# Down projection of a decoder layer by seven half-size products, from forms of ff kept in DRAM

## The chip, the cores and the metric

The kernel runs on one core of one Trainium2 chip. The metric is the device time of one execution in microseconds (us): the median of three runs of the kernel before is 2154.42 us (2153.45 to 2158.33).

## The reference, cut to what matters

One layer (d_model 2048, 512 tokens, float32): a norm, three parallel mixers (attention, convolution, a gated recurrence), their common output projection and the residual; then the part that the change touches:

```python
h  = x + concat(mixers) @ w_out
n  = rms_norm(h, ffn_norm_w)
ff = silu(n @ w_gate) * (n @ w_up)          # 2048 -> 5632
y  = h + ff @ w_down                        # 5632 -> 2048
out = rms_norm(y, final_norm_w)
```

The output must agree in float32. One matmul in the fast format of TensorE keeps too few bits, so each operand is split into a high and a low part, and each product is three matmuls (high by high, high by low, low by high).

## The kernel before, in words

Everything after the mixers is held with channels as partitions and the 512 tokens as columns. The mixers end at about 600 us of the span. Four stages follow.

**Project** (`project`, L667). 16 tiles of `h` (128 channels x 512 tokens), each from 48 matmuls of 512 columns. Each tile is added to x on VectorE (DVE), stored to DRAM (`hd`) from ScalarE's queue, and split into `hh`, `hl` (scaled by ffn_w); GpSimd (POOL) adds up its squares in `acc`. `project_end` turns the sums into `rstd` and `rms`.

**Sums of n** (`token_sums`, L701). DVE builds four sums and differences of quarters of n, split as well; the seven half-size products of gate/up use them as the stationary operand.

**Gate/up.** ff has 44 tiles (128 channels x 512 tokens). The first two are computed plainly (`ff_plain`), the other 42 by Winograd's form of Strassen's scheme (`ff_fast`): seven products `11`, `12`, `S2`, `S1`, `S3`, `22`, `S4`, each 24 matmuls of 256 columns, in place of eight. A block of weights is a raw tile of 128 x 1024; ScalarE (ACT) casts it into `wh` (L136), DVE subtracts and gives `wl` (L137). The finished tile is stored to DRAM (`ffd`), 256 KB, on SyncE's queue (SP).

**Down** (`down_all`, L886). Five chunks of eight k-tiles and a last one of four. ACT's queue loads ff tiles from `ffd`, ACT and DVE split them (`fh`, `fl`), and each of 16 output tiles takes 24 matmuls of 512 columns per chunk, 1920 in all; DVE adds each to `h` (L813). The last chunk goes by halves of the tokens, 384 matmuls of 256 columns, with the final norm (`down_last`); POOL does a part of the last scaling (L860, L861).

The order on each engine is written down when the kernel is built, by a scheduler with priorities: what stands in `high_priority` is moved ahead as far as buffers allow. At run time each engine takes its list in order. A DMA is an entry of the list of the engine that issues it, and an entry that waits holds up all behind it.

Of the kernel before, what the change touches and what calls it, by code (L numbers as in the profile page):

```python
# [27 lines left out]
GF = 4  # L28
CF = 8
NCHUNK = NF // CF  # L30
PLAIN = 2
HALF = 256
NB = S // P
# [11 lines left out]
POOL_OUT = (0, 4)  # L45
# [8 lines left out]
def _layout_cols():  # L54
    at = 0
    for name, n in (
        ("attn_w", 16), ("q_w", 4), ("kv_w", 4), ("mla_w", 1), ("conv_w", 4 * CONV_W),
        ("conv_b", 4), ("ln_w", 4), ("ln_b", 4), ("lower", HG), ("hgrn_w", 1),
        ("ffn_w", 16), ("final_w", 16), ("inv_freq", 1), ("sign", 1), ("eps", 1),
        ("ln_eps", 1), ("half_pi", 1),  # L60
    ):
        _COLS[name] = (at, n)
        at += n
    return at
# [28 lines left out]
class Trunk:  # L93
# [573 lines left out]
    def project(self, w, r4):  # L667
# [3 lines left out]
        self.hd = self.dp.tile([KT, P, S], F32, name="hd")  # L671
        sq_sum = self.sq_sum = r4("acc")
        for m in range(KT):
            t = self.hf[:, m]
            nc.sync.dma_start(t, self.io["x"][m])
            bank = self.cols_tile(w, self.mix_y + self.mix)
            nc.vector.tensor_tensor(t, t, bank, op=ALU.add)
            nc.scalar.dma_start(self.hd[m], t)
            self.hw.append(self.split(t, self.hp("hh", F32R), self.hp("hl", F32R), self.col("ffn_w", m)))
            if m == 0:  # L680
                nc.scalar.activation(sq_sum, t, AF.Square)
            else:
                q = r4("sq")
                nc.scalar.activation(q, t, AF.Square)
                nc.gpsimd.tensor_tensor(sq_sum, sq_sum, q, op=ALU.add)
            nc.scalar.activation(t, t, AF.Copy, scale=self.col("ffn_w", m))

    def project_end(self, r4):
# [3 lines left out]
        y, q, v = r4("sq"), r4("sq"), r4("acc")  # L692
        nc.vector.tensor_scalar(self.rms, total, 1.0 / D, self.col("eps"), op0=ALU.mult, op1=ALU.add)
        r = self.rsqrt(total, D, "eps", v, y, q)
        nc.vector.tensor_scalar(self.epsv, self.rms, EPS, None, op0=ALU.mult)
        nc.vector.tensor_tensor(self.rms, self.rms, r, op=ALU.mult)
        nc.vector.tensor_copy(self.rstd, r)
# [28 lines left out]

    def put_ff(self, f, g, u):
# [4 lines left out]
        nc.sync.dma_start(self.ffd[f], u)  # L732

    def ff_plain(self, f, w, fp):
        nc = self.nc
        gbank = self.cols_tile(w, self.hw)
        ubank = self.cols_tile(w, self.hw)
        g, u = fp("g"), fp("u")
# [3 lines left out]
        nc.sync.dma_start(self.ffd[f], u)  # L742

    def ff_fast(self, f, w, rp, fp):
# [4 lines left out]
        with self.tc.high_priority(offset=6000):  # L749
            b11, b21, b12, b22 = raws = [rp("raw", F32, W) for _ in range(4)]  # L750
            for t in raws:
                nc.sync.dma_start(t, next(w))
# [19 lines left out]
        g, u = fp("g"), fp("u")  # L772
# [7 lines left out]
        def sums():  # L780
            tt(b11, b12, b11, op=ALU.subtract)
            t2 = rp("t2", F32, W)
# [16 lines left out]
        self.put_ff(f, g, u)  # L799


    def ff_load(self, k, fp):
        nc = self.nc
        with self.tc.high_priority(offset=3000):
            t = fp("fr")
            nc.scalar.dma_start(t, self.ffd[k])
            return self.split(t, fp("fh", F32R), fp("fl", F32R))

    def down(self, w, ff):
        nc = self.nc  # L810
        for m in range(KT):
            bank = self.cols_tile(w, ff)
            nc.vector.tensor_tensor(self.h[:, m], self.h[:, m], bank, op=ALU.add)  # L813

    def down_last(self, w, ff, r5, lp):

        nc = self.nc
        self.tables_after(self.last_silu)
        wt = []
        for m2 in range(KT // 2):  # L820
            if m2 < 3:
                h, l = self.weights(next(w))
                wt += [(h[:, :S], l[:, :S]), (h[:, S:], l[:, S:])]
            else:
                raw = self.wp.tile([P, 1024], F32, tag="raw", name="raw", bufs=2)
                nc.sync.dma_start(raw, next(w))
                for s in (slice(0, S), slice(S, 2 * S)):
                    wt.append(self.split(raw[:, s], lp("wlh", F32R), lp("wll", F32R)))
        n = S // 2
        acc = r5("acc")  # L830
        for th in range(2):
            ts = slice(th * n, (th + 1) * n)
            for m in range(KT):
                bank = self.ps("mm")[:, :n]
                for k in range(GF):
                    s = slice(k * P, (k + 1) * P)
                    self.mm3(bank, (wt[m][0][:, s], wt[m][1][:, s]), (ff[k][0][:, ts], ff[k][1][:, ts]),
                             k == 0, k == GF - 1)
                hm = self.h[:, m, ts]
                nc.vector.tensor_tensor(hm, hm, bank, op=ALU.add)  # L840
                if m == 0:
                    nc.scalar.activation(acc[:, ts], hm, AF.Square)
                else:
                    q = r5("sq", F32, (P, n))
                    nc.scalar.activation(q, hm, AF.Square)
                    nc.vector.tensor_tensor(acc[:, ts], acc[:, ts], q, op=ALU.add)
            scaled = {}
            for m in POOL_OUT:
                scaled[m] = o = lp("mx")
                for i in range(2):  # L850
                    nc.scalar.activation(o[:, i * n:(i + 1) * n], self.h[:, m + i, ts], AF.Copy,
                                         scale=self.col("final_w", m + i))
            bank = self.ps("ax")[:, :n]
            nc.tensor.matmul(bank, self.ones, acc[:, ts], start=True, stop=True)
# [255 lines left out]
```

## Time and profile before

| | |
|---|---|
| median of three runs | 2154.42 us |
| profiled execution, its own time | 2154.74 us |
| its span | 2153.0 us |
| PE busy | 2100.1 us (98%) |
| DVE busy | 1391.3 us (65%) |
| ACT busy | 891.2 us (41%) |
| POOL busy | 172.2 us (8%) |
| moved by DMA | 252.43 MB, 117 GB/s |

How to read it: busy time is summed over the instructions of an engine; PE is TensorE's matmuls. A busy share over the whole span mixes stages, so the table by stage below is the one to use. Instructions of one engine overlap a little at their ends, so a chain of n like ones takes less than n times the mean of one.

### The profile page before, as it was taken

The numbers are of one execution on the slowest core, as the hardware profiler recorded it, in microseconds if no ns is written. First come the engines' busy times: TensorE is split into PE (matmuls) and PEld (weight loads), VectorE is DVE, ScalarE is ACT, GpSimd is POOL, SyncE is SP. The second block draws the span as 40 slices with busy tenths as digits, with TensorE's granted clock in tenths as the row PEclk, the third lists the DMA queues.
The fourth block names the chain that finished last, engine by engine and source line by source line (L and its number), as shares of the span: only waits on it lengthen the run. The fifth ranks groups of instructions, "written<-read, shape, count | busy, mean of one in ns | idle before, by whom it ended". The sixth has DMA issues, their size and how long they took to land.

```text
span 2153.0 us, 31933 instructions
## 1 busy us (share of the span) xinstructions
PE 2100.1 (98%) x13060; PEld 1893.8 (88%) x13060; DVE 1391.3 (65%) x1787; ACT 891.2 (41%) x1353; POOL 172.2 (8%) x152
## 2 busy tenths in 40 slices
PE   8999999999999999999999999999997999999997
PEld 6888888878878789999999999999996788888887
DVE  7897785556543377777777778777776443443447
ACT  6324763457543344444444444444443222221223
POOL 4102474100011100000000000000000000000001
PEclk9999999999999999999999999999999999999998
DMA  5233422222153333433433433443335443342333
GB/s 186 96 118 98 143 80 87 90 83 79 63 187 122 123 122 114 133 111 111 133 116 106 133 122 104 128 129 106 120 123 181 137 137 103 132 135 94 100 107 98
DMA packets 89907, 252.43 MB, mean 117 GB/s; under 512 B 9424, under 2 KB 17872, under 8 KB 89760
## 3 DMA queue, kind: packets, MB, share of 16 engines
q1 hardware_dynamic: 76528, 228.00, 33.0%
q10 hardware_dynamic: 13120, 22.03, 2.9%
q8 instruction: 102, 1.67, 0.3%
q0 software_dynamic: 112, 0.36, 0.1%
q14 instruction: 45, 0.37, 0.1%
HBM read 226.24 MB, written 24.12 MB: 116 GB/s over the span
## 4 chain that ended last, share of the span: by engine, by line
PE 90%; ACT 3%; DVE 3%; DMA 2%; POOL 1%; issue 1%; SPq 0%; DVEq 0%; ACTq 0%; POOLq 0%
PE mm L145 28%; PE mm L146 28%; PE mm L147 28%; PE lv L374 1%; PE ob L615 1%; DMA xraw<-in_x 1%; PE lv L145 1%; PE lv L147 1%; PE lv L146 1%; DVE mx L866 1%; ACT wh L136 1%; DMA fr<-ffd 0%; PE tb L607 0%; POOL ps L364 0%; DMA raw<-in_w_down 0%
## 5 line engine op out<-in xcount | busy, mean ns | idle before, releaser
L136 ACT CAST wh<-raw 128x1024 fp32r<-128x1024 f32 (+1 forms) x463 | 478.2, 1034 | 834.7 <-PE mm L146 762.4
L137 DVE TENSOR_TENSOR wl<-raw,wh 128x1024 fp32r<-128x1024 f32 (+1 forms) x463 | 568.0, 1228 | 330.1 <-ACT wh L136 329.8
L146 PE MATMUL mm<-sl,wh 128*128 128x256 f32 x1344 | 378.3, 283 | 0.0
L145 PE MATMUL mm<-sh,wh 128*128 128x256 f32 x1344 | 378.1, 283 | 0.0
L147 PE MATMUL mm<-sh,wl 128*128 128x256 f32 x1344 | 373.5, 283 | 0.0
L145 PE MATMUL mm<-hh,wh 128*128 128x256 f32 (+1 forms) x1072 | 308.0, 287 | 0.0
L146 PE MATMUL mm<-hl,wh 128*128 128x256 f32 (+1 forms) x1072 | 307.5, 287 | 0.0
L147 PE MATMUL mm<-hh,wl 128*128 128x256 f32 (+1 forms) x1072 | 307.3, 287 | 0.0
L145 PE MATMUL mm<-fh,wh 128*128 128x512 f32 (+1 forms) x688 | 262.8, 386 | 12.8 <-ACT fh L136 9.7
L146 PE MATMUL mm<-fl,wh 128*128 128x512 f32 (+1 forms) x688 | 264.1, 384 | 0.2 <-DVE fl L137 0.2
L147 PE MATMUL mm<-fh,wl 128*128 128x512 f32 (+1 forms) x688 | 263.5, 383 | 0.0
L145 PEld LDWEIGHTS mm<-sh,wh 128*128 128x128 f32 x1344 | 257.3, 191 | 0.2 <-DVE u L794 0.2
L146 PEld LDWEIGHTS mm<-sl,wh 128*128 128x128 f32 x1344 | 257.5, 192 | 0.0
L147 PEld LDWEIGHTS mm<-sh,wl 128*128 128x128 f32 x1344 | 254.7, 192 | 0.0
L813 DVE TENSOR_TENSOR h<-h,mm 128x512 f32<-128x512 f32 x80 | 54.8, 687 | 236.2 <-PE mm L147 236.2
L146 PEld LDWEIGHTS mm<-hl,wh 128*128 128x128 f32 x1072 | 202.2, 189 | 3.0 <-issue 0.5
L145 PEld LDWEIGHTS mm<-hh,wh 128*128 128x128 f32 x1072 | 201.7, 188 | 3.4 <-issue 0.5
L147 PEld LDWEIGHTS mm<-hh,wl 128*128 128x128 f32 x1072 | 201.8, 188 | 2.9
L145 PE MATMUL mm<-xh,wh 128*128 128x512 f32 x400 | 160.1, 400 | 6.1 <-ACT wh L136 5.9
L145 PEld LDWEIGHTS mm<-fh,wh 128*128 128x128 f32 x688 | 130.4, 190 | 38.8 <-ACT fh L136 9.9
L146 PE MATMUL mm<-xl,wh 128*128 128x512 f32 x400 | 158.2, 396 | 0.5 <-DVE xl L140 0.5
L147 PE MATMUL mm<-xh,wl 128*128 128x512 f32 x400 | 157.0, 396 | 0.0
(330 smaller groups left out, 3236.6 us busy)
## 6 DMA issues: line engine op xcount, KB each, us to landing
raw<-in_w_gu SPq DMA_DIRECT2D x176, 512.0 KB, 4.2
raw<-in_w_down SPq DMA_DIRECT2D x88, 512.0 KB, 3.3
raw<-in_w_cols SPq DMA_DIRECT2D x42, 512.0 KB, 3.4
raw<-in_w_out SPq DMA_DIRECT2D x32, 512.0 KB, 3.3
ffd<-u SPq DMA_DIRECT2D x44, 256.0 KB, 3.8
fr<-ffd ACTq DMA_DIRECT2D x44, 256.0 KB, 3.7
raw<-in_w_rows SPq DMA_DIRECT2D x16, 512.0 KB, 3.3
raw<-in_w_attn SPq DMA_DIRECT2D x14, 512.0 KB, 3.4
```

The source lines that it names most:

```text
L136: nc.scalar.copy(h, src)
L137: nc.vector.tensor_tensor(l, src, h.bitcast(F32), op=ALU.subtract)
L145: mm(out, a[0], b[0], start=first, stop=False, **k)
L146: mm(out, a[0], b[1], start=False, stop=False, **k)
L147: mm(out, a[1], b[0], start=False, stop=last, **k)
L374: nc.tensor.matmul(bank[:, c * 64:(c + 1) * 64], e[:, c * P:(c + 1) * P], ap_of(e, c * P + h, [2 * h, 64 // h], [1, h]), start=True, stop= ...
L615: nc.tensor.matmul(obank[:, qs], pt[:, js], vt[h // 4, j][:, hs], start=j == 0, stop=j == i)
L813: nc.vector.tensor_tensor(self.h[:, m], self.h[:, m], bank, op=ALU.add)
L866: nc.vector.scalar_tensor_tensor(o[:, i * n:(i + 1) * n], self.h[:, m + i, ts], self.col("final_w", m + i), r, ALU.mult, ALU.mult)
```

## The change: what it does

`h` is now needed with tokens as partitions. In project, each `h` tile is transposed by four TensorE transposes (`turn`), copied by ACT and stored to `hd`; the gate tile of f = 0 stands ahead of `project_end`. In gate/up, two neighbouring ff tiles lie side by side in one tile `form`; `put_forms` makes of them the seven operands of down's products (four subtractions or additions of 128x256), casts them (`fh`, 128x1792) and takes the low part in place, and stores both, 0.92 MB each, where before two tiles of 256 KB were stored. The tiles `u`, `pb`, `g` and the raw tiles have other numbers of buffers.

Down is new (`down_all`, `down_block`). ff (tokens) is the stationary operand, w_down's sums move with 512 columns. Four chunks of 6, 6, 6 and 4 pairs of k-tiles, each done for two halves `mb` of the output: eight blocks of seven products. Per chunk the 14 tiles of forms are loaded by SP; per block 6 or 4 times n raw tiles of w_down (128x1024) come in, of which POOL and DVE make sums. The accumulators `acc` (four tiles of 128x2048) are loaded from `hd` by ACT's queue, and products are added into them by DVE. The final norm works on rows of tokens. In short:

```diff
     def project(self, w, r4):
         for m in range(KT):
-            t = self.hf[:, m]
+            t = r4("h")
             bank = self.cols_tile(w, self.mix_y + self.mix)
+            if m:
+                self.turn(m - 1, prev, r4)
             nc.vector.tensor_tensor(t, t, bank, op=ALU.add)
-            nc.scalar.dma_start(self.hd[m], t)
...
+    def turn(self, m, t, r4, tag="tb"):
+        bank = self.ps(tag)
+        for c in range(NB):
+            s = slice(c * P, (c + 1) * P)
+            nc.tensor.transpose(bank[:, s], t[:, s], self.ident)
+        o = r4("t")
+        nc.scalar.copy(o, bank)
+        nc.scalar.dma_start(self.hd[:, :, m * P:(m + 1) * P].rearrange("c p f -> p c f"),
+                            o.rearrange("p (c f) -> p c f", c=NB))
...
+    def put_forms(self, j, fp):
+        x = self.form
+        at = lambda i: x[:, i * HALF:(i + 1) * HALF]
+        tt = nc.vector.tensor_tensor
+        tt(at(4), at(1), at(3), op=ALU.add)
+        tt(at(1), at(0), at(1), op=ALU.subtract)
+        tt(at(5), at(4), at(0), op=ALU.subtract)
+        tt(at(6), at(2), at(5), op=ALU.subtract)
+        h = fp("fh", F32R, (P, 7 * HALF))
+        l = x[:].bitcast(F32R)
+        nc.scalar.copy(h, x)
+        tt(l, x, h.bitcast(F32), op=ALU.subtract)
+        for part, t in enumerate((h, l)):
+            nc.sync.dma_start(self.ffd[part, :, :, j * HALF:(j + 1) * HALF].rearrange("f p c -> p f c"),
+                              t.bitcast(F32).rearrange("p (f c) -> p f c", f=7))
...
+    def load_forms(self, at, n, tp):
+        with self.tc.high_priority(offset=3000):
+            for name in ("11", "12", "S2", "S1", "S3", "22", "S4"):
+                for part in range(2):
+                    t = tp(f"{name}{'hl'[part]}", F32R, (P, n * HALF))
+                    self.nc.sync.dma_start(t.bitcast(F32), self.ffd[part, FORMS[name], :, at * HALF:(at + n) * HALF])
...
+    def down_block(self, w, A, n, mb, rp, add, last=False):
+        product(one, b11, "11")
+        put((0, 0), one)
+        product(two, b21, "12")
+        put((0, 0), two)
+        def sums(i):
+            tg(b11[i], b12[i], b11[i], op=ALU.subtract)
+            t2 = self.wp.tile([P, 1024], F32, tag="raw", name="raw", bufs=2)
+            tv(t2, b22[i], b11[i], op=ALU.subtract)
+            tv(b21[i], t2, b21[i], op=ALU.subtract)
+            tg(b12[i], b22[i], b12[i], op=ALU.subtract)
+            return t2
+        product(one, Sums(), "S2", start=False)
...
     def run(self):
-        fp = area("gu", {"g": 2, "u": 2, "pa": 2, "pb": 2, "pc": 2}, "right")
+        fp = area("gu", {"g": 1, "form": 1, "fh": 1, "pa": 2, "pb": 1, "pc": 2}, "right")
-        rp = area("raw4", {"raw": 5, "t2": 1}, "right")
+        rp = area("raw4", {"raw": 4}, "right")
```

(`tg` is GpSimd, `tv` VectorE.) Three places where the lists of the engines change. The numbers behind names are buffer numbers; `L` is the line of the kernel that the row belongs to (in the new kernel the cast is L135 and its subtraction L136).

First, ACT's list at the start of down. Before, loads of `hd` and of ff and casts of ff alternate:

```order
L891 DMA h_16116<-hd_5009 128x512
L806 DMA fr_16150<-ffd_6188 128x512
L119 ACT_TABLE_LOAD
L806 DMA fr_16156<-ffd_6188 128x512
L136 CAST fh_16146<-fr_16144 128x512
```

Now the casts of the first nine raw tiles and the last pair's `fh` come, then the four loads of the accumulators, then the next casts:

```order
L770 CAST fh_16371<-form_15925 128x1792
L135 CAST wh_16515<-raw_16439 128x1024
L135 CAST wh_16531<-raw_16441 128x1024
L135 CAST wh_16547<-raw_16443 128x1024
L135 CAST wh_16570<-raw_16566 128x1024
L135 CAST wh_16591<-raw_16587 128x1024
L135 CAST wh_16612<-raw_16608 128x1024
L951 DMA acc_16392<-hd_5006 128x2048
L951 DMA acc_16393<-hd_5006 128x2048
L951 DMA acc_16394<-hd_5006 128x2048
L951 DMA acc_16395<-hd_5006 128x2048
L135 CAST wh_16630<-raw_16433 128x1024
```

The four accumulator loads now stand between the casts of product S2 and those of S1; `acc_16392` uses the memory of `form` and `fh`, so it comes after the two stores below.

Second, SP's list there. Before, the last ff tile is stored ahead of all but two of the weights of down:

```order
L732 DMA ffd_6188<-u_15660 128x512
L130 DMA raw_16319<-in_w_down 128x1024
L130 DMA raw_16351<-in_w_down 128x1024
L732 DMA ffd_6188<-u_15889 128x512
L130 DMA raw_16383<-in_w_down 128x1024
L130 DMA raw_16415<-in_w_down 128x1024
```

Now the stores of the last pair's two parts stand behind 12 raw tiles and the 14 loads of forms:

```order
L873 DMA raw_16455<-in_w_down 128x1024
L857 DMA 11h_16405<-ffd_6388 128x1536
L857 DMA 11l_16407<-ffd_6388 128x1536
L857 DMA 12h_16409<-ffd_6388 128x1536
L857 DMA 12l_16411<-ffd_6388 128x1536
L857 DMA S2h_16413<-ffd_6388 128x1536
```

```order
L857 DMA S4h_16429<-ffd_6388 128x1536
L857 DMA S4l_16431<-ffd_6388 128x1536
L773 DMA ffd_6388<-fh_16371 128x7x256
L773 DMA ffd_6388<-form_15925 128x7x256
L873 DMA raw_16832<-in_w_down 128x1024
```

Between these two pieces stand the other loads of forms; the two stores moved from the head of the queue to the end of these 26 loads.

Third, DVE's list in gate/up, where one ff tile ends and the next begins. Before (the first three rows are the subtractions of products 22 and S4, and of product 11 of the next tile):

```order
L137 TENSOR_TENSOR wl_11235<-raw_11068,wh_11234 128x1024
L137 TENSOR_TENSOR wl_11264<-raw_11070,wh_11263 128x1024
L137 TENSOR_TENSOR wl_11314<-raw_11296,wh_11313 128x1024
L794 TENSOR_TENSOR u_11080<-pc_11083,mm_11077 128x256
L781 TENSOR_TENSOR raw_11296<-raw_11298,raw_11296 128x1024
```

Now, at every second such place:

```order
L766 TENSOR_TENSOR form_9893<-form_9893 128x256
L136 TENSOR_TENSOR wl_10512<-raw_10345,wh_10511 128x1024
L767 TENSOR_TENSOR form_9893<-form_9893 128x256
L136 TENSOR_TENSOR wl_10541<-raw_10347,wh_10540 128x1024
L771 TENSOR_TENSOR form_9893<-form_9893,fh_10339 128x1792
L136 TENSOR_TENSOR wl_10589<-raw_10572,wh_10588 128x1024
L841 TENSOR_TENSOR g_10356<-pc_10360,mm_10355 128x256
L826 TENSOR_TENSOR raw_10572<-raw_10574,raw_10572 128x1024
```

The forms' work stands between the subtractions that the products wait for, and the wide one (L771) waits for ACT's cast `fh_10339`.

## Rows read from the trace of the kernel before

**Rows 1.** The page's chain that ended last, shares of the span

```profile
PE 90%; ACT 3%; DVE 3%; DMA 2%; POOL 1%; issue 1%; SPq 0%; DVEq 0%; ACTq 0%; POOLq 0%
```

**Rows 2.** By stretch: length, PE, PEld, DVE, ACT, POOL busy (count); clock, DMA, GB/s

```profile
570.00:746.00 176.00, 172.97 (x797) 143.45 (x795) 70.10 (x100) 74.68 (x128) 20.23 (x14) 0.99 0.40 136
800.00:1636.00 836.00, 835.98 (x7025) 835.78 (x7024) 635.32 (x707) 359.67 (x461) 0.00 (x0) 1.00 0.37 117
1637.00:1672.00 35.00, 22.01 (x81) 16.59 (x79) 23.12 (x35) 12.73 (x19) 0.00 (x0) 0.82 0.76 271
1672.00:2060.00 388.00, 388.00 (x1710) 321.10 (x1710) 157.40 (x177) 93.59 (x102) 0.00 (x0) 1.00 0.36 119
2137.00:2153.00 16.00, 0.70 (x2) 0.30 (x2) 9.02 (x18) 1.67 (x4) 3.56 (x4) 0.62 0.40 131
```

**Rows 3.** PE's waits, 1600 to 1700: released by; us, times, longest

```profile
PE mm L145 <- ACT fh L136: 9.7, 1, 9.7
PE mm L145 <- ACT wh L136: 3.0, 1, 3.0
```

**Rows 4.** Timeline of PE: start, us, what; project's mixers and stage ends

```profile
581.85 0.60 PE L639 MATMUL tb<-ident,og 128*128 128x128 f32 x4
582.29 0.27 PE L607 MATMUL tb<-ident,p 128*128 128x128 f32 x1
...
1314.31 0.28 PE L145 MATMUL mm<-hh,wh 128*128 128x256 f32 x1
...
1637.24 0.28 PE L147 MATMUL mm<-sh,wl 128*128 128x256 f32 x1
1647.26 1.65 PE L145 MATMUL mm<-fh,wh 128*128 128x512 f32 x3 [9.74 <-ACT fh L136]
...
2136.64 0.28 PE L147 MATMUL mm<-fh,wll 128*128 128x256 f32 x1
```

**Rows 5.** PE's waits, 740 to 800

```profile
PE mm L197 <- POOL acc L685: 4.0, 1, 4.0
```

**Rows 6.** DVE and ACT groups: shapes, count; busy us, mean ns; idle before

```profile
L137 DVE TENSOR_TENSOR wl<-raw,wh 128x1024 fp32r<-128x1024 f32 x447 | 552.8, 1237 | 329.3 <-ACT wh L136 329.1
L813 DVE TENSOR_TENSOR h<-h,mm 128x512 f32<-128x512 f32 x80 | 54.8, 687 | 236.2 <-PE mm L147 236.2
L794 DVE TENSOR_TENSOR u<-pc,mm 128x256 f32<-128x256 f32 x42 | 17.4, 414 | 0.0
L136 ACT CAST wh<-raw 128x1024 fp32r<-128x1024 f32 x447 | 469.0, 1050 | 833.9 <-PE mm L146 762.4 <-PE lv L147 26.1 <-PE mm L147 24.5
```

**Rows 7.** Timeline of DVE at an end of a gate/up tile

```profile
1309.76 1.23 DVE L137 TENSOR_TENSOR wl<-raw,wh 128x1024 fp32r<-128x1024 f32 x1 [1.42 <-ACT wh L136]
1312.87 1.23 DVE L137 TENSOR_TENSOR wl<-raw,wh 128x1024 fp32r<-128x1024 f32 x1 [1.89 <-ACT wh L136]
1314.02 0.41 DVE L794 TENSOR_TENSOR u<-pc,mm 128x256 f32<-128x256 f32 x1
```

**Rows 8.** The page's DMA issues: KB each, median us to landing

```profile
ffd<-u SPq DMA_DIRECT2D x44, 256.0 KB, 3.8
```

**Rows 9.** By stretch at down's start, columns as in rows 2

```profile
1644.00:1648.00 4.00, 0.74 (x2) 0.65 (x3) 1.08 (x2) 1.06 (x2) 0.00 (x0) 0.50 1.06 411
1652.00:1656.00 4.00, 4.00 (x17) 3.22 (x17) 4.00 (x8) 1.03 (x2) 0.00 (x0) 0.90 0.91 336
```

**Rows 10.** Timelines of DVE and POOL, early in the kernel and in project

```profile
24.86 2.43 DVE L140 SCALAR_TENSOR_TENSOR xl<-xraw,cols,xh 128x512 fp32r<-128x512 f32 x2
25.44 1.30 POOL L273 TENSOR_TENSOR acc<-acc,xsq 128x512 f32<-128x512 f32 x1 [2.26 <-ACT xsq L272]
27.82 0.74 DVE L140 SCALAR_TENSOR_TENSOR xl<-xraw,cols,xh 128x512 fp32r<-128x512 f32 x1
```

**Rows 11.** Timeline of the tail, after the last matmul

```profile
2142.17 6.71 DVE L866 SCALAR_TENSOR_TENSOR mx<-h,cols,v 128x256 f32<-128x256 f32 x12
2143.55 5.73 SPq L883 DMA_DIRECT2D out_y<-mx  x4
```

More of the change, by code (lines that the diff above doesn't have):

```diff
@@ L749, in ff_fast @@
         with self.tc.high_priority(offset=6000):
-            b11, b21, b12, b22 = raws = [rp("raw", F32, W) for _ in range(4)]
+            extra = lambda: self.wp.tile([P, 1024], F32, tag="raw", name="raw", bufs=2)
+            b11, b21, b12, b22 = raws = [extra()] + [rp("raw", F32, W) for _ in range(3)]
             for t in raws:
@@ new lines, in down_block, with load, early, parts @@
+    def down_block(self, w, A, n, mb, rp, add, last=False):
+        nc = self.nc
+        W = (P, 1024)
+        units = range(n // 2)
+        def load():
+            with self.tc.high_priority(offset=6000):
+                out = []
+                for _ in units:
+                    t = rp("raw", F32, W)
+                    nc.sync.dma_start(t, next(w))
+                    out.append(t)
+                return out
+        def early(f, *a):
+            with self.tc.high_priority(offset=6000):
+                return f(*a)
+        def parts(t):
+            h, l = (self.wp.tile([P, 1024], F32R, tag=x, name=x) for x in ("wh", "wl"))
+            return self.split(t, h, l)
+        def product(banks, ts, name, start=True, by_sub=False):
+            mine = A[name]
+            def step(b, hl, i, p):
+                s = slice(p * S, (p + 1) * S)
+                k = 2 * i + p
+                x = slice(k * HALF + b * P, k * HALF + (b + 1) * P)
+                self.mm3(banks[b], (mine[0][:, x], mine[1][:, x]), (hl[0][:, s], hl[1][:, s]),
+                         start and k == 0, k == n - 1, skip_group_check=not start)
+            if by_sub:
+                hls = [early(parts, ts[i]) for i in units]
+                for b in range(2):
+                    for i in units:
+                        for p in range(2):
+                            step(b, hls[i], i, p)
+                return
+            for i in units:
+                hl = early(lambda: parts(ts[i]))
+                for p in range(2):
+                    for b in range(2):
+                        step(b, hl, i, p)
+        b11, b21, b12, b22 = (load() for _ in range(4))
+        two_banks = lambda: [self.ps("mm") for _ in range(2)]
+        one, two, three, four = (two_banks() for _ in range(4))
+        def put(q, banks, op=ALU.add):
+            for b in range(2):
+                add(q, b, banks[b], op)
+        tv, tg = nc.vector.tensor_tensor, nc.gpsimd.tensor_tensor
+        product(one, b11, "11")
[9 more added lines that the diff above has]
+            return t2
+        class Sums:
+            def __getitem__(_, i):
+                return sums(i)
+        product(one, Sums(), "S2", start=False)
+        put((0, 1), one)
+        product(three, b11, "S1")
+        put((1, 1), three)
+        product(one, b12, "S3", start=False)
+        put((1, 0), one)
+        put((1, 1), one)
+        product(four, b21, "22")
+        put((1, 0), four, ALU.subtract)
+        product(three, b22, "S4", start=False, by_sub=last)
+        put((0, 1), three)
@@ L969, in run @@
         tp = area("sum", {"s": 1}, "right")
-        self.ffd = self.dp.tile([NF, P, S], F32, name="ffd")
-        wg = stream("w_gu")
+        self.ffd = self.dp.tile([2, 7, P, NP * HALF], F32, name="ffd")
         self.token_sums(sp, tp)
```

215 lines of the change are left out of this document (97 added, 118 removed).

## The prediction, made before the changed kernel ran

> **What bounds the kernel now.** I read the chain that ended last first: it is PE for 90% of the span [rows 1]. The table by stretch then says where PE still waits. In gate/up it never does, and its 7025 matmuls of 256 columns take 836 us, 0.119 us each; in the middle of down it doesn't either: 1710 matmuls of 512 columns in 388 us, 0.2269 us each; in project it works 173 of 176 us [rows 2]. It waits at the seams: 4.0 us for POOL's sum of squares ahead of the norm [rows 5], and at down's start 9.7 and 3.0 us [rows 3], with the clock granted at 0.50 (1.2 GHz) for a while after [rows 9]. So an edit counts here in two ways only: by how many matmuls PE is given, and by what it does to the seams. DVE is the second engine: 635 of 836 us in gate/up [rows 2].
>
> **The change part by part.** The sum is made against the profiled execution, 2154.74 us (0.3 above the median, 1.7 above its span).
>
> *Matmuls of down: -62.0.* Before, 1920 of 512 columns (435.6 us at 0.2269) and 384 of 256 (45.7 at 0.119): 481.3. After, 22 pairs x 7 products x 2 token tiles x 2 halves of the output x 3 = 1848 of 512 columns: 419.3. All on PE's path.
>
> *Transposes: +7.* 16 tiles by four. In the stream of matmuls before, four f32 transposes go by in 0.44 us (581.85 to 582.29 [rows 4]): 16 x 0.44 = 7.0. One by itself lasts 0.27 [rows 4], so unpipelined it would be 17.3; below 7 it can't go, since PE is full there. I take the pipelined end, because they stand between matmuls here too. ACT's copies and the stores lie beside PE's 11 us per tile.
>
> *The seam after project: +3 (-2 to +6).* The gate tile of f = 0 now stands ahead of the norm's sums and covers the 4.0 us. But `token_sums` also waits until the last transposed tile has been copied and stored (its memory is reused), some 9 us later by the new order, and the first fast product needs blocks that wait behind those sums. The two nearly cancel; I take +3.
>
> *Gate/up: +8 (0 to +40).* Per pair of tiles DVE gets four additions of 128x256 (0.41, [rows 6]) and one of 128x1792; by the shapes (1.237 at 1024, 0.414 at 256, so 0.0011 per element [rows 6]) the wide one takes about 2.05. That is 3.5 us more per 40, on 30: room in sum. The place matters. Before, the last subtraction of a tile (S4) starts 4.55 us ahead of the next tile's first matmul, and the next tile's first subtraction 1.44 us ahead [rows 4, 7]. Now two additions and the wide subtraction stand around S4's, and the wide one waits for ACT's cast of 1792 (1.05 x 1.75 = 1.8 us, [rows 6]), which starts only when the last addition is done, at about -4.5. So cast until -2.7, wide subtraction until -0.7, first subtraction of the next tile until +0.5, where the low part is wanted at about +0.2: PE waits some 0.4 us, in 20 pairs 8 us. If that cast is earlier it is nothing. The upper end: `form` has one buffer, and the next pair's first write to it (L839) waits for the landing of the low part's store, which is issued at the end of the wide subtraction, some 6.5 us earlier. A store of 256 KB lands after 3.8 us [rows 8]; 0.92 MB at 336 to 411 GB/s [rows 9] takes 2.2 to 2.7 us and lands after 5 to 6.6 by these rows. Just hidden; if not, some 2 us per pair.
>
> *Down's start: +24.9 (+18 to +32).* Before, from the last matmul of gate/up at 1637.24 to the last of down at 2136.64 are 499.4 us [rows 4], for 481.3 of work: 18.1 lost, nearly all at the start. Now count from gate/up's end, T = 0. SP's list there: 11 raw tiles that could not start earlier (5.77 MB, from about -4.8, when product 22 of the last tile lets go of memory), 14 forms (11.0 MB), the last pair's two stores (1.8 MB), all in one queue. At 375 GB/s, the middle of 336 and 411 [rows 9], the raws are through at 10.6, the first two forms at 14.8, with landing 17: PE stands still until T = 17 (before: 10.0). Then products 11 and 12, 16.3 us, a part of it at the lower clock. At that start before, the first three matmuls took 1.65 us [rows 4]; I take 2.5 us for it, so PE is done with both at 36. The third product, S2, adds onto the bank of the first, and that has to be put into the accumulator, which is loaded by ACT from `hd` only once both stores have landed: their memory is the accumulator's. 18.6 MB at 375 GB/s are through at 45, landed at 47; the first accumulator (1.05 MB) at 51.5, the second at 54.3; S2 starts at about 55. ACT, which issues those loads, stands still with them, so the casts for product S1 come late too, another 1.8. Lost: 55 less 16.3 of work, plus 2.5 for the lower clock once more after this second stand and the 1.8, is 43.0 against 18.1. At 336 GB/s S2 starts at 60, at 411 at 50.
>
> *The rest of down: +6 (0 to +25).* A block of n = 6 has PE for 252 x 0.2269 = 57.2 us. DVE has 21 subtractions and 6 sums of 128x1024 and 16 additions of 128x512: in a row, at 1.14 and 0.60 us (a tenth under the lone means of [rows 6]), 40.4 us. But POOL has six sums of 128x1024 there, and POOL gets in DVE's way: two operations that need 0.74 us each took 2.43 while POOL's 1.30 us addition ran [rows 10]. They take turns. POOL's for 1024 columns is about 2.6 (twice 1.30), so DVE and POOL in turn need 40.4 + 15.6 = 56.0 of 57.2; for n = 4 it is 30.1 + 10.4 = 40.5 of 38.1. The load is also uneven: until the last unit of S2 starts, 21.8 us into the block, 14 of DVE's (16.0), four additions (2.4) and four of POOL's (10.4) have to be done, 28.8. With three buffers for `wh` the work can start up to 5.4 us ahead, so 1.6 us too few per block at worst, and additions that read PSUM may not take turns. I take 0.8 for each of the seven blocks behind the first, whose long wait lets DVE run ahead.
>
> The Trainium skill says the same of that turn-taking ("SBUF — State Buffer", section "SBUF: two separate sides"): the ports which GpSimd shares with VectorE are held by one for a whole instruction, when VectorE has two inputs in SBUF. By that rule the trace agrees (2.43 for 1.48), and it speaks against giving POOL sums in down; it also leaves out the additions from PSUM, which would make the term the smaller one.
>
> *Tail: -1.7.* Before, 2153.0 - 2136.64 = 16.4 us. After: an addition (0.69), the small chain (2), eight scalings of 128x1024 at 1.14 (9.1) and a store of 512 KB (about 3): 14.7. The chain before was of the same kind: 12 scalings, and the stores among them [rows 11].
>
> Sum: 2154.7 - 62.0 + 7 + 3 + 8 + 24.9 + 6 - 1.7 = 2139.9, forecast 2140 us.
>
> **The rivals.**
>
> *A, the accumulators don't hold PE up.* If the stores or loads go sooner than their place in the queue says, S2 starts at 36, and 19 us of the loss are gone: 2121, and with the seams of gate/up hidden 2116. For it: transfers are spread over 16 engines, which before ran at a share of 1.06 at 411 GB/s [rows 9]. Against: the list of ACT has the loads ahead of the next casts, and the stores are last of 28 entries.
>
> *B, gate/up is held by its stores.* L839 comes just behind the landing. If the store, in pieces of 1 KB, takes 2 us longer than I reckon, every pair loses 2 us: 40 in place of 8, 2172. It decides from 1.1 us per pair (8 + 14.8 us in 20 pairs), slower than before beyond. For it: one buffer for `form` and `fh`, the margin is under 1.5 us. Against: traffic is low in gate/up, 117 GB/s [rows 2].
>
> *C, DVE and POOL in turn become the bound of down.* If also PSUM additions take turns, or the sums don't start ahead, a block loses up to 28.8 - 21.8 = 7 us; at 4 in seven blocks it is 28 in place of 6, 2162. It is slower than before from 2.9 us per block. For it: 56.0 of 57.2. Against: DVE in project is seen beside POOL only in small pieces, and PSUM reads may go free.
>
> **How the numbers follow.** What can be told from no change is 0.2%, 4.3 us: faster is under 2150.1, slower over 2158.7. Forecast 0.58 (own range 2126 to 2154), A 0.14, B 0.12, C 0.16. Faster: A and most of the forecast (0.50): 0.64. Same: 0.10, the forecast's upper edge and C's lower. Slower: B, C and the rest: 0.26. The range, 2117 to 2166, leaves out the far parts of B and C and half of A's lower end.
>
> **What would show it.** In project, four transposes per tile between matmuls, 0.44 us; if PE's gaps there grow, the first term is wrong. In gate/up, PE idle about 0.4 us per pair with the releaser `wl`; a wait of DVE for the landing of `ffd` at L839 would be B. At down's start, PE idle 17 us, working 19, then idle about 19 with the releaser an `acc` addition at L966, and ACT idle until the stores land; if the second gap is missing, A. In the blocks behind, PE idle for `wl` under 1 us per block; DVE subtractions stretched from 1.2 to over 3 us beside POOL, and PE waiting for them by several us in product S2, would be C. The forecast is wrong if PE's matmuls of down don't number 1848, or if the second gap is under 10 or over 30 us.

## The result, and the profile after

The changed kernel takes 2183.76 us (median of four runs, 2182.11 to 2185.25) against 2156.38 for the kernel before on the same chip: a ratio of 1.0125 (95% interval 1.0104 to 1.0146). The forecast was 2140, faster; it came out slower, above the range given. The profiled execution took 2185.25 us, its span is 2183.5. One execution of all the runs below was a slow one (2547.39 us, mean granted clock 0.748 where the others have 0.97 to 0.99), the profiled one of the first experiment, and no number below uses it.

The page of the changed kernel, first the busy times, then the chain that ended last, which answers to [rows 1]:

```profile
PE 2063.5 (95%) x12672; PEld 1842.1 (84%) x12672; DVE 1627.1 (75%) x1925; ACT 974.7 (45%) x1393; POOL 301.8 (14%) x188
PE 76%; DVE 10%; issue 5%; DMA 4%; ACT 3%; POOL 1%; SPq 0%; DVEq 0%; POOLq 0%; ACTq 0%
```

PE is busy 36.6 us less than before (2100.1), and yet the span is 30.5 longer. Its part of the chain fell from 90% to 76%, and DVE's rose from 3% to 10%: the end is now set by what PE waits for. The timeline of PE at the stage ends (start, duration, what) says where, set against [rows 4]:

```profile
803.40 0.28 PE L144 MATMUL mm<-hh,wh 128*128 128x256 f32 x1
1657.59 0.28 PE L146 MATMUL mm<-sh,wl 128*128 128x256 f32 x1
1672.75 0.77 PE L144 MATMUL mm<-wh,11h 128*128 128x512 f32 x1 [14.88 <-DMA 11h<-ffd]
1708.51 0.77 PE L144 MATMUL mm<-wh,S2h 128*128 128x512 f32 x1 [16.24 <-issue]
2167.68 0.39 PE L146 MATMUL mm<-wh,S4l 128*128 128x512 f32 x1
```

Between these starts and those of before:

| stretch | before | after | difference | predicted |
|---|---|---|---|---|
| start to the end of project | 745.7 | 755.1 | +9.4 | +7 |
| to the first matmul of 256 columns (the two plain tiles lie in it) | 51.6 | 48.3 | -3.3 | +3 |
| gate/up, the 42 fast tiles | 839.9 | 854.2 | +14.3 | +8 |
| down | 499.4 | 510.1 | +10.7 | -31.1 (-62.0 + 24.9 + 6) |
| tail | 16.4 | 15.8 | -0.5 | -1.7 |
| sum | 2153.0 | 2183.5 | +30.5 | -14.8 |

So 42 of the 45 us that the forecast was short lie in down. What PE waits for there, in the table of waits from 1640 to the end (us, times, longest), where before had the two waits of [rows 3]:

```profile
PE mm L145 <- DVE wl L136: 39.6, 16, 5.3
PE mm L144 <- issue: 16.2, 1, 16.2
PE mm L144 <- DMA 11h<-ffd: 14.9, 1, 14.9
```

The two long waits are those of down's start, and were predicted (17 and 19). The second of them is put down to "issue", where the profile shows nothing that PE waited for; DVE's timeline does, since the addition that frees the bank waited for the accumulators' loads:

```profile
1707.66 0.75 DVE L966 SCALAR_TENSOR_TENSOR acc<-acc,rms,mm 128x512 f32<-128x512 f32 x1 [13.01 <-DMA acc<-hd]
```

The first row of the waits is the new one: 39.6 us for DVE's subtractions. The stretches show it too (columns as in [rows 2]): the middle of gate/up, and the end of a block with the head of the next.

```profile
820.00:1620.00 800.00, 790.26 (x6638) 782.16 (x6637) 672.28 (x768) 374.18 (x452) 0.00 (x0) 1.00 0.46 151
1740.00:1800.00 60.00, 53.36 (x226) 43.34 (x224) 46.84 (x37) 19.84 (x19) 18.91 (x6) 0.94 0.51 181
```

In the second, PE stands for 6.6 of 60 us and its mean granted clock is 0.94, where [rows 2] had 1.00 and no idle time. DVE isn't full in it, 46.84 of 60. The timelines of DVE and of POOL in that stretch say why it is late all the same:

```profile
1752.05 0.67 DVE L968 TENSOR_TENSOR acc<-acc,mm 128x512 f32<-128x512 f32 x1
1752.65 2.82 DVE L925 TENSOR_TENSOR raw<-raw 128x1024 f32<-128x1024 f32 x1
...
1759.86 3.41 DVE L925 TENSOR_TENSOR raw<-raw 128x1024 f32<-128x1024 f32 x1
1763.20 3.40 DVE L926 TENSOR_TENSOR raw<-raw 128x1024 f32<-128x1024 f32 x1
1766.52 3.35 DVE L136 TENSOR_TENSOR wl<-raw,wh 128x1024 fp32r<-128x1024 f32 x1
...
1771.11 1.21 DVE L926 TENSOR_TENSOR raw<-raw 128x1024 f32<-128x1024 f32 x1
```

```profile
1748.64 2.40 POOL L923 TENSOR_TENSOR raw<-raw 128x1024 f32<-128x1024 f32 x1 [65.21 <-DVE wl L136]
1751.13 3.27 POOL L927 TENSOR_TENSOR raw<-raw 128x1024 f32<-128x1024 f32 x1
...
1762.16 6.64 POOL L927 TENSOR_TENSOR raw<-raw 128x1024 f32<-128x1024 f32 x2
```

POOL does its six sums in a row, in 20 us, once per block. In that time an operation of DVE with two inputs in SBUF takes up to 3.3 to 3.4 us in place of 1.2, just as long as one of POOL's: the two go in turn, one for one. The additions from PSUM (L968, 0.67) are not stretched, beside POOL or not. POOL's burst falls on the head of the block, where DVE has to give the sums and the low parts of two products. PE pays twice in each block of six pairs (the last row is the first place of the next block):

```profile
1758.86 0.50 PE L145 MATMUL mm<-wl,11h 128*128 128x512 f32 x1 [1.31 <-DVE wl L136]
1769.93 0.79 PE L145 MATMUL mm<-wl,12h 128*128 128x512 f32 x1 [5.33 <-DVE wl L136]
1825.28 0.50 PE L145 MATMUL mm<-wl,11h 128*128 128x512 f32 x1 [1.32 <-DVE wl L136]
```

A block lasts 66.4 us from one such place to the next (1758.86 to 1825.28; 65.7 to 66.9 in the others) for 57.2 of matmuls. 6.6 of the loss is waiting; most of the other 2.6 us is the lower clock behind the long wait, granted at 0.50 (1.2 GHz) for 3.4 us (columns as in [rows 2]):

```profile
1770.00:1773.40 3.40, 3.40 (x8) 2.72 (x9) 3.40 (x5) 0.00 (x0) 0.00 (x0) 0.50 0.00 0
```

### The profile page after: what moved, and what is told of

Read it like the earlier page. It is cut to its first block, busy times and chain, and to the rows that moved or that the text cites. A ratio compares the mean times of both kernels' runs of the same rounds, so it can differ in the third digit from the quotient of the medians.

```text
span 2183.5 us, 31515 instructions
## 1 busy us (share of the span) xinstructions
PE 2063.5 (95%) x12672; PEld 1842.1 (84%) x12672; DVE 1627.1 (75%) x1925; ACT 974.7 (45%) x1393; POOL 301.8 (14%) x188
## 4 chain that ended last, share of the span: by engine, by line
PE 76%; DVE 10%; issue 5%; DMA 4%; ACT 3%; POOL 1%; SPq 0%; DVEq 0%; POOLq 0%; ACTq 0%
PE mm L146 23%; PE mm L145 23%; PE mm L144 23%; DVE wl L136 4%; DMA ffd<-form 2%; DVE form L771 1%; ACT wh L135 1%; PE lv L373 1%; PE ob L614 1%; DVE raw L926 1%; DMA xraw<-in_x 1%; DVE raw L925 1%; PE lv L145 1%; PE lv L144 1%; PE lv L146 1%
## 5 line engine op out<-in xcount | busy, mean ns | idle before, releaser
L135 ACT CAST wh<-raw 128x1024 fp32r<-128x1024 f32 (+1 forms) x576 | 594.7, 1038 | 956.4 <-PE mm L145 425.3
L136 DVE TENSOR_TENSOR wl<-raw,wh 128x1024 fp32r<-128x1024 f32 (+1 forms) x576 | 731.2, 1278 | 351.4 <-ACT wh L135 347.5
L923 POOL TENSOR_TENSOR raw<-raw 128x1024 f32<-128x1024 f32 x22 | 66.8, 3040 | 1235.4 <-DMA raw<-in_w_down 903.4
L144 PE MATMUL mm<-mx,wh 128*128 128x512 f32 x256 | 101.0, 398 | 0.8 <-ACT mx L138 0.8
L146 PE MATMUL mm<-mx,wl 128*128 128x512 f32 x256 | 100.9, 395 | 0.0
L145 PE MATMUL mm<-mx,wh 128*128 128x512 f32 x256 | 100.8, 394 | 0.0
L144 PEld LDWEIGHTS mm<-xh,wh 128*128 128x128 f32 x400 | 76.5, 191 | 23.0 <-ACT wh L135 5.8
```

Of the source, the lines that this page charges most:

```text
L135: nc.scalar.copy(h, src)
L136: nc.vector.tensor_tensor(l, src, h.bitcast(F32), op=ALU.subtract)
L144: mm(out, a[0], b[0], start=first, stop=False, **k)
L145: mm(out, a[0], b[1], start=False, stop=False, **k)
L146: mm(out, a[1], b[0], start=False, stop=last, **k)
L923: tg(b11[i], b12[i], b11[i], op=ALU.subtract)
```

## The experiments

Theory 1: the loss per block comes from POOL and DVE taking turns at SBUF. Its rivals, as the expectations number them: theory 2, DVE has too much to do at the head of the block, whatever POOL does; theory 3, the raw tiles come late. A question apart from these is the second stand at down's start: does it come from the place of the last two stores in SP's queue, as predicted? T is the end of gate/up, as in the prediction. Runs given without an interval are single ones.

**All sums of w_down on DVE.**

```diff
-        tv, tg = nc.vector.tensor_tensor, nc.gpsimd.tensor_tensor
+        tv = tg = nc.vector.tensor_tensor
```

> Edit: all four sums of w_down's blocks on VectorE, none on GpSimd. Theory 1 (GpSimd and VectorE take turns at SBUF, so GpSimd's sums hold up the subtractions that PE waits for): the VectorE rows beside the sums fall from 3.3 to 1.2 us, the waits of PE for wl of 1.3 and 5.3 us per block go, the period of a block with n = 6 falls from 65.7-66.9 us to about 57.5, of n = 4 from 42.2 to about 38.5, the time to about 2184 - 5 x 8.7 - 2 x 4 = 2132. Theory 2 (VectorE has too much to do, unevenly, in the first three products, whatever GpSimd does): six more sums of 1.14 us at that place make the waits longer, period 70 us or more, time 2190 or more. Theory 3 (the raw tiles of w_down come late): nothing changes, 2184.

Measured: 2134.88 us (three executions), 0.9898 of before (0.9881 to 0.9915): 48.9 us less than the changed kernel, and faster than the kernel before by 1%. Theory 2 (2190 or more) and theory 3 (no change) are out by this. The trace is that of the same kernel, run once more:

> The kernel of e1 once more, for its profile. Theory 1 as there: period of a block with n = 6 about 57.5, VectorE's rows beside the sums 1.2 us, no wait of 1.3 and 5.3 us; time 2135.

2130.6 us (its part ahead of gate/up was some 7 us shorter than in the changed kernel, by chance: nothing differs there). Of PE's waits, one over 0.3 us is left in each block of six pairs, in product S2:

```profile
1759.04 0.50 PE L145 MATMUL mm<-wl,S2h 128*128 128x512 f32 x1 [0.85 <-DVE wl L136]
1817.81 0.50 PE L145 MATMUL mm<-wl,S2h 128*128 128x512 f32 x1 [0.84 <-DVE wl L136]
```

DVE by groups in this kernel, from 1710 to 2120 (count; busy us, mean ns; idle before):

```profile
L136 DVE TENSOR_TENSOR wl<-raw,wh 128x1024 fp32r<-128x1024 f32 x143 | 172.7, 1221 | 68.9 <-ACT wh L135 68.9
L925 DVE TENSOR_TENSOR raw<-raw 128x1024 f32<-128x1024 f32 x19 | 23.1, 1217 | 0.0
```

And the same groups in the changed kernel, from 1710 to 2167:

```profile
L136 DVE TENSOR_TENSOR wl<-raw,wh 128x1024 fp32r<-128x1024 f32 x145 | 203.9, 1412 | 92.4 <-ACT wh L135 90.6 <-DMA 22h<-ffd 1.5
...
L925 DVE TENSOR_TENSOR raw<-raw 128x1024 f32<-128x1024 f32 x19 | 45.4, 2389 | 0.5
```

With more work given to DVE the block is shorter, 58.8 in place of 66.4 us, and every operation is back at 1.22. From S2's start to the last matmul it is 414.4 us (1698.36 to 2112.75) in place of 459.2. The edit also changes the order of DVE's list and in which PE takes the products at the head of a block; the run with POOL's idle work, below, has the order of this one.

**Half of the sums back on POOL** (b11's on DVE, b12's on POOL).

```diff
-            tg(b11[i], b12[i], b11[i], op=ALU.subtract)
+            tv(b11[i], b12[i], b11[i], op=ALU.subtract)
```

> Edit: the first of the four sums (b11) on VectorE, the last one (b12, needed only for product S3) stays on GpSimd. Theory 1: half of GpSimd's time is gone, and the first product's chain no longer goes through GpSimd; the waits per n = 6 block fall to about 2 us, period about 60, time about 2145 to 2155. Theory 2: 2184 or more.

2164.87 us. In PE's waits in down the row of the subtractions is now this one:

```profile
PE mm L145 <- DVE wl L136: 23.7, 12, 2.4
```

It lies between the two, as the theory has it, but the time is 10 us over the upper end. A block takes 62.8 to 64.3 us. Three of POOL's operations in place of six take away a third of the loss per block, not half or more; why is not shown.

**POOL does work that nobody reads**: the sums on DVE as above, and two subtractions of 128x1024 per unit on POOL, into a tile of its own.

```diff
-        tv, tg = nc.vector.tensor_tensor, nc.gpsimd.tensor_tensor
+        tv = tg = nc.vector.tensor_tensor
...
+            for _ in range(2):
+                nc.gpsimd.tensor_tensor(self.junk, b22[i], b22[i], op=ALU.subtract)
```

> Edit: e1 (all sums on VectorE), and beside it two additions of 128x1024 per unit on GpSimd, as many as GpSimd had in the change, whose result nobody reads. Theory 1 (turns at SBUF): PE's waits for wl at the head of each block come back although nothing waits for GpSimd's results; time 2165 to 2195 (e1: 2135). Theory 1b (the chain through GpSimd's sums is what is late: 3.3 us each, handed on to t2 and the split of S2): the waits stay away, 2135 to 2140.

2180.75 us: 46 of the 49 us are back, though nothing waits for POOL's results and the lists at the head of the block are in the order of the kernel without POOL's work. PE, DVE and POOL of this kernel, each from its timeline:

```profile
1829.16 0.80 PE L145 MATMUL mm<-wl,11h 128*128 128x512 f32 x1 [7.61 <-DVE wl L136]
```

```profile
1748.11 2.91 DVE L136 TENSOR_TENSOR wl<-raw,wh 128x1024 fp32r<-128x1024 f32 x1
1756.61 0.67 DVE L970 TENSOR_TENSOR acc<-acc,mm 128x512 f32<-128x512 f32 x1
1760.04 2.35 DVE L136 TENSOR_TENSOR wl<-raw,wh 128x1024 fp32r<-128x1024 f32 x2
```

```profile
1741.55 16.89 POOL L929 TENSOR_TENSOR junk<-raw 128x1024 f32<-128x1024 f32 x6 [29.95 <-DMA raw<-in_w_down]
```

While POOL is busy (until 1758.4) DVE's subtraction takes 2.91 us; after that two take 2.35. The addition from PSUM takes 0.67 in the middle of it. So the cost lies in the two engines at SBUF at the same time, and not in the chain of sums through POOL, nor in the order.

**The last pair's two stores on ACT's queue**, the sums as in the changed kernel.

```diff
+        q = nc.scalar if j == NP - 1 else nc.sync
-            nc.sync.dma_start(self.ffd[part, ...
+            q.dma_start(self.ffd[part, ...
```

> Edit: the last pair's two stores of ff's forms are issued from ScalarE's queue instead of SyncE's, so they don't stand behind 26 loads. If the place in SyncE's queue is what delays the accumulators (prediction): the stores land some 15 to 25 us earlier, product S2 of the first block starts about 36 us after the end of gate/up in place of 50.9, time -12 to -17. If the transfers as a whole are the limit (16 engines shared): the loads of the forms are late in turn, S2 starts at 45 or later, time -6 or less.

2178.93 us, but none of the difference is where it was looked for: S2 starts at T + 49.9 (before this edit 50.6), and gate/up began 3 us earlier with unchanged code ahead of it. The stores' issues, first in the changed kernel, from SP, then in this one, from ACT:

```profile
1684.83 0.37 SPq L773 DMA_DIRECT2D ffd<-fh  x1
1686.73 0.37 SPq L773 DMA_DIRECT2D ffd<-form  x1
```

```profile
1667.23 0.37 ACTq L774 DMA_DIRECT2D ffd<-fh  x1
1678.08 0.37 ACTq L774 DMA_DIRECT2D ffd<-form  x1
```

The second store was issued only at 1678.08, 17 us after its data was ready and within 0.1 us of the landing of a form (S2l), just as SP's issues in this stretch come one by one behind landings. It landed at T + 44.1, in the changed kernel at T + 44.8. So the edit didn't bring the stores forward, and can't tell whether their place matters. This edit and the first one (sums on DVE) together:

> Edit: e1 and e3 together. Theory 1 and the queue's place: the two gains lie in different stretches and add up, about 2184 - 51 - 14 = 2119, below the kernel before. If the first block's long stand was what let VectorE run ahead in block 2, a few us less.

2138.37 us, 0.9909 of before (0.9893 to 0.9926), S2 at T + 50.6: ACT's queue is worth nothing, on either footing. The DMA is busy throughout, at 410 to 422 GB/s from 3 to 35 us behind T, as two windows of the changed kernel show (from 3 and from 27 us behind T; the last columns are clock, DMA share and GB/s). What is left to try is what stands ahead of the stores:

```profile
1661.00:1665.00 4.00, 0.00 (x0) 0.00 (x0) 3.38 (x6) 1.80 (x2) 0.35 (x1) 0.59 1.04 422
1685.00:1689.00 4.00, 4.00 (x20) 3.30 (x19) 3.96 (x4) 1.25 (x2) 0.00 (x0) 1.00 1.02 416
```

**The forms of the first chunk that are not needed yet (S1, S3, 22, S4), behind those two stores**, the sums on DVE.

```diff
+        names = ("11", "12", "S2", "S1", "S3", "22", "S4")
+        soon = 7 if at else 3
...
+            get(names[:soon])
...
+            get(names[soon:], True)
```

(`True` puts these loads behind the last store.)

> Edit: e1, and of the first chunk's 14 loads of forms the eight of S1, S3, 22 and S4 stand behind the last pair's two stores in SyncE's list. What is ahead of the accumulators falls by 6.3 MB, 15 us at the 415 GB/s of the trace. If the bytes ahead set the start of S2 (51 us after gate/up's end in the changed kernel): it starts at 36 to 38, time 2135 - 13 = 2122. If the accumulators wait for something else: S2 stays at 50, 2135.

2130.06 us, 0.9881 of before (0.9865 to 0.9898). S2 at T + 42.6, a little more than half of the gain expected (T is 1654.20):

```profile
1696.85 0.76 PE L144 MATMUL mm<-wh,S2h 128*128 128x512 f32 x1 [8.55 <-issue]
```

The two stores landed at T + 27.0 and T + 29.3, 15.5 us sooner than in the changed kernel: so their place in SP's list does matter. The accumulators' loads were issued from 1685.76 on, but took 8.4 to 14.6 us to land (4.9 to 11.0 in the changed kernel), beside the eight loads of forms that now came at the same time: the load that is waited for shares the rate with those put behind it.

**Cast and low part of the forms in two pieces** (1024 and 768 columns), on top of that.

```diff
+        a, b = slice(0, 4 * HALF), slice(4 * HALF, 7 * HALF)
+        nc.scalar.copy(h[:, a], x[:, a])
...
+        for s in (a, b):
+            tt(l[:, s], x[:, s], h[:, s].bitcast(F32), op=ALU.subtract)
```

> Edit: e6, and in gate/up the cast and the low part of the forms in two pieces (1024 and 768 columns), so that the first piece's cast runs beside two of the additions. If the wait of VectorE for the wide cast is what PE's 6.9 us of wl waits in gate/up come from: these go, VectorE's low part is stored about 1 us sooner and the waits at form (4.6 us) shrink, gate/up takes 845 instead of 854 us, time 2122 - 8 = 2114. If VectorE's load as such (83%) is the cause: no change, 2122.

2133.89 us, 0.990 of before (0.9886 to 0.9915): a miss. PE's waits in gate/up, first of the changed kernel (800 to 1640), then of this one:

```profile
PE mm L146 <- DVE wl L136: 6.9, 21, 1.6
PE mm L144 <- DVE form L839: 4.6, 6, 1.1
PE mm L144 <- ACT wh L135: 0.4, 1, 0.4
```

```profile
PE mm L144 <- ACT wh L135: 16.1, 19, 0.8
PE mm L146 <- DVE wl L136: 2.0, 1, 2.0
```

The wait for DVE is gone as meant, and one for ACT has come in its place. It is not the wide casts that hold that cast up: before the wait of PE at 909.47 they end at 899.07, while the cast PE waits for starts at 908.38, released by a matmul. Why the order came out so is open.

**Neither cast nor low part** (forms behind as before, casts and low part not split): the wide cast and the wide subtraction are left out of gate/up, and both stores take `form` as it is.

```diff
-        h = fp("fh", F32R, (P, 7 * HALF))
-        nc.scalar.copy(h, x)
-        tt(l, x, h.bitcast(F32), op=ALU.subtract)
-        for part, t in enumerate((h, l)):
+        for part, t in enumerate((l, l)):
```

> Edit: e6, but in gate/up the wide cast and the wide low part of the forms are left out (both stores take the same tile, so the result of down is not ff's). If these two are what costs gate/up its 14 us over the kernel before (854.3 against 840.0): PE's waits for wl at the ends of tiles (6.9 us) go, gate/up takes about 845, time 2130 - 9 = 2121. If the four additions and VectorE's load are the cause: 852 or more, 2129.

2117.15 us. Gate/up lasts 837.1 us (803.63 to 1640.69), and PE's waits in it are these:

```profile
PE mm L146 <- DVE wl L136: 1.7, 1, 1.7
PE mm L144 <- ACT wh L135: 0.4, 1, 0.4
```

The additions and both stores are still in it, so the waits hang on the wide cast and its subtraction (11.9 us, now 2.1); the stores, issued earlier, cost PE nothing. The waits explain 9.8 of the 17 us, but a wait costs more than its idle time: matmuls around it are slow as well. In gate/up of the changed kernel 114 matmuls start more than 0.15 us behind the one before, here 58; over 0.119 us each, these places cost 25.5 and 9.8 us, waits included, so the difference is 15.7 us.

**The accumulators in memory of their own.** Two of the four lay where `form` and `fh` were. Now two lie apart and are loaded by ACT at once, the other two by SP; the sums on DVE. First alone, then with the forms behind:

```diff
-        acc = self.acc = [ap("acc", F32, (P, D)) for _ in range(NB)]
+        acc = self.acc = [a("acc", F32, (P, D)) for a in ap for _ in range(2)]
-            nc.scalar.dma_start(acc[c], self.hd[c])
+            (nc.scalar if c < 2 else nc.sync).dma_start(acc[c], self.hd[c])
...
+        a1 = area("acc1", {"acc": 2}, "right")
```

> Edit: e1, and the two areas for the accumulators as in e10, the order of the forms as in the change. If the accumulators' wait for the last pair's stores is what the second stand is made of (16 us in the change): it goes, S2 starts at 39 to 41 after gate/up's end in place of 50.6, time 2135 - 10 = 2125. If not, 2135 or more.

> Edit: e6, and the accumulators in two areas of memory: the two that product 11 and S2 need lie where only the first stage's operands lay and are loaded by ScalarE's queue without waiting for the last pair's stores; the other two are loaded by SyncE's queue behind the forms. If the wait for these stores still holds S2: the second stand of PE (8.6 us in e6) goes; but 2.1 MB more are ahead of the first forms, 5 us, so product 11 starts at 20 us instead of 15 and S2 at about 39 to 40 after gate/up's end (e6: 42.6). Time 2130 - 3 = 2127. If the bytes of the forms behind are what slows the loads: the same start of S2 as e6, 2130.

2123.24 us alone; 2122.59 with the forms behind, 0.9843 of before (0.9827 to 0.9859), the best kernel here: faster than before by 1.6%. PE's waits in down in the latter:

```profile
PE mm L144 <- DMA 11h<-ffd: 20.8, 1, 20.8
PE mm L145 <- DVE wl L136: 4.2, 5, 0.8
```

The second stand is gone (S2 at T + 37.9 and T + 40.0), against 5 to 6 us more of the first: two accumulators, 2.1 MB, now run ahead of form `11`, 5 us at 415 GB/s. So what held PE the second time was the accumulators' loads, which waited for the two stores. Moving the forms behind is worth nothing more by then (a single run against four).

**Cast and low part made in down** (one store and one load of the forms in f32, halving their traffic; `form` gets a second buffer), sums on DVE and accumulators as above.

```diff
-        nc.scalar.copy(h, x)
-        tt(l, x, h.bitcast(F32), op=ALU.subtract)
...
+                self.nc.scalar.copy(h, l.bitcast(F32))
+                self.nc.vector.tensor_tensor(l, l.bitcast(F32), h.bitcast(F32), op=ALU.subtract)
```

> Edit: e11, and the forms are stored and loaded once in float32; the cast and the low part are made when they are loaded in down (seven of 128x1536 per chunk), none in gate/up; form gets a second buffer. If e9's 13 us were the cast and low part standing in gate/up's way: gate/up at 845 or less; down's start has 5.5 + 0.9 MB less to move, S2 starts at 36 to 38 after gate/up's end; VectorE in down has 7 x 1.7 = 12 us more per chunk, on 47 of 57 per block, which should fit in the blocks with n = 6. Time 2123 - 12 - 3 = 2108. If down's VectorE can't take it, the waits for wl per block come back, 2 to 4 us in each chunk's two blocks: 2115 to 2123.

2130.19 us, 0.988 of before (0.9861 to 0.9899): a miss. Gate/up falls to 829.9 us, but down takes 481.4 in place of 450.9. Its waits there:

```profile
PE mm L144 <- ACT 11h L851: 22.2, 1, 22.2
PE mm L145 <- DVE wl L136: 13.5, 14, 2.6
PE mm L144 <- ACT wh L135: 7.3, 12, 1.2
```

The cast of the first form now follows its load, and the forms' casts and subtractions stand between those of w_down, so that the block waits come back from another cause.

## Why the prediction was wrong, by its own steps

**The step that failed is "The rest of down: +6 (0 to +25)".** From S2's start to the last matmul are 459.2 us for 1776 matmuls of 0.2269 (403.0): 56.2 lost, where the prediction had 6, and 4.3 for the clock and the casts after the second stand. The same stretch without POOL's sums loses 11.4 (414.4 - 403.0), almost what was predicted; so POOL's share is 44.8. The mechanism was in the text as rival C, at 4 us a block and a chance of 0.16. It was seen, and mis-sized in these ways:
- *The head start.* Without it the text had 28.8 - 21.8 = 7 us a block; it took off 5.4 for the three `wh` buffers, and then half of the rest. PE's waits are 6.6 us in each of five blocks of six pairs and 3.2 in each of two of four, 39.6 in all: nearly the 7 without that credit.
- *The place.* The text held the work against one point, the start of S2's last unit. PE waits earlier, 7.4 and 18.4 us into the block (it starts at 1751.50): DVE's list has two of the sums (1759.86 and 1763.20) ahead of the low part that product 12 needs (1766.52), and beside POOL these three take 10.2 us in place of 3.7.
- *What follows a wait.* The text put nothing behind these waits; a block of six pairs lasts 2.6 us more than its matmuls and waits, most of it the lower clock.

Two other errors cancel. Four of POOL's sums were reckoned to fall ahead of S2's last unit, and all six do; 2.6 us were reckoned for each on top of DVE's own time, and in turn a pair takes 3.3, where DVE alone takes 1.2. From 1750.06 to 1769.87 seven operations of DVE take 19.0 us in place of 8.5, so POOL takes 10.5 us from DVE there; the text had 10.4.

The sum over the block (56.0 of 57.2 us) came near, with DVE busy for 52.5 us from 1751.50 to 1817.91, its turns included. A sum over a block says nothing when the work falls in its head. Of the Trainium skill ("SBUF — State Buffer", section "SBUF: two separate sides") the rule that the shared ports are held for a whole instruction, where VectorE has two inputs in SBUF and GpSimd reads there, is borne out: the trace agrees that such operations are held up (3.3 in place of 1.2), and that those with one input in PSUM, which the rule leaves out, are not (0.67).

**Transposes, +7: right.** Each four cost 0.46 us between matmuls (the first four 0.79); 14 of the 16 lie in that stretch, 6.8 us. The other 2.5 us of it stand already ahead of project, in code that is the same.

**The seam, +3: -3.3.** The gate tile of f = 0 covers the whole wait of [rows 5], and the wait for the last transposed tile is not seen: between 755 and 803 PE is busy for 47.57 of 48 us.

**Gate/up, +8: +14.3, near by luck.** The place was right: 21 waits for `wl` of 0.33 us, 6.9 us, against 0.4 in 20 pairs (DVE's added work per pair is 3.7 us by the text's own terms, not 3.5, which changes nothing). What was left out is a piece of rival B, 4.6 us in six waits of PE at L839. And a wait costs more than its idle time: the waits, 12 us, and the slow matmuls around them come to 25.5 (counted in the experiment without cast and low part). Little of that is the clock, which was granted at 0.50 for 3 us from 812.2 on and at 1.00 in the mean from 820 to 1640. Some 11 us came back where nothing was forecast: the products on `hh` and `hl` run faster than before (last section). DVE's own waits in gate/up have the store behind L839:

```profile
DVE form L839 <- DMA ffd<-form: 6.9, 7, 1.4
```

The store is late in a third of the pairs, not in all, by 1 us: its landing takes 6.4 us at the median, at the upper end of the 5 to 6.6 reckoned.

**Down's start, +24.9: about 16, by the mechanism that was forecast.** Of the 24.9, 4.3 were reckoned behind S2's start; until it, 20.6 were forecast, and 16.2 came (50.6 - 16.3 = 34.3 lost, against 18.1 before). The first stand is 14.9 for 17. The stores landed at T + 42.5 and T + 44.8 for 47, ACT issued the accumulators right behind the second, and S2 started at T + 50.6 for 55, once the first of them was in. The difference is the rate, 410 to 422 GB/s for the 375 taken (by 411 the text had 50). The reason given was the place of the two stores behind 26 loads, and the runs bear it out: with eight of these loads behind them the stores landed 15.5 us sooner and S2 came 8 us sooner. That their move to ACT's queue changed nothing doesn't speak against it, since the second store landed no sooner. A memory of their own for two accumulators took the stand away. Rival A, that the accumulators don't hold PE up, was wrong for this kernel.

**Matmuls of down, -62: right.** 1848 by 0.2269. **Tail, -1.7: -0.5.**

Set right, the sum is: -62 + 9.4 - 3.3 + 14.3 + 16.2 + 56.2 - 0.5 = +30.3, of +30.5 measured. With the sums on DVE the same change brings 1%, some 22 us, with the accumulators apart as well 1.6%: what was predicted of the seven products is there, and POOL's 44 sums (138 us of its time) cost twice what then remains.

## What to carry to other kernels

Before giving POOL a share of DVE's work, look for an operation of DVE with two inputs in SBUF beside one of POOL's in the trace: here it ran at POOL's pace, and six sums per block taken off DVE made DVE later. Additions that read one input from PSUM were not touched. Reckon an engine's load at the place in the loop where its results are due, not over the loop's length. Where a load waits for memory that a store must leave first, look at what stands ahead of that store: here other memory for the load helped most, fewer loads ahead of the store helped in part, and another engine's queue didn't, because the issue was held there too.

## What the runs showed that was not expected

- Seemingly full stretches of gate/up differ between kernels though PE never idles and the matmuls are the same. The middle 800 us of the last experiment (columns as in [rows 2]):

```profile
820.00:1620.00 800.00, 800.00 (x6828) 800.00 (x6827) 650.53 (x775) 348.56 (x446) 0.00 (x0) 1.00 0.38 129
```

  That is 0.1172 us a matmul, where the kernel before has 0.119 [rows 2], at the same granted clock. Its gate/up is 10 us shorter than that of the kernel before. The difference lies in the products that have `hh` and `hl` as stationary operand, 3024 of the 7056 matmuls: they follow each other in 0.114 us, in the changed kernel too, and in 0.118 in the kernel before; the others take 0.120 in all three. The change lays `hh` and `hl` into two groups of buffers each; what sets the pace was not tried.
- DMA of one core moved 410 to 422 GB/s for some 30 us of loads (374 to 400 where the two stores end), and a load of 0.79 MB then took 10.8 to 15.9 us to land, with seven others issued ahead of it and still under way.
- The part ahead of gate/up varied by up to 8 us between runs of the same code (first gate/up matmul at 795.86 to 803.63). Differences of a few us between single runs above are read from their stages for that reason.
